# Recurrence level products as paired 64-column halves, both live units in one block ahead of the probability-value batch

## The chip, the cores and the metric

The kernel runs on one core of a Trainium2 chip. TensorE (PE in the profile, its weight loads PEld) multiplies matrices into PSUM; VectorE (DVE) and ScalarE (ACT) read PSUM and SBUF; GpSimd (POOL) works on SBUF; SyncE (SP) issues the DMAs here. Each engine runs its own queue in order and waits on semaphores for the others. The metric is the device time of one execution in microseconds.

## The reference, cut to what matters

One transformer layer over 2048 latent tokens with 256 context tokens in front: a modulated norm, one input projection, two groups of heads side by side, an output projection, then a feed-forward part. The change lies where the two groups of heads are computed together:

```python
# (A) softmax attention: 8 query heads, 2 key/value heads, 128-query blocks, 2304 keys
s = einsum('bqkgd,bnkd->bkgqn', q, keys) * scale;  p = softmax(s);  o = einsum('bkgqn,bnkd->bqkgd', p, vals)
# (B) gated linear recurrence: 4 heads of 128 x 128, forward and backward, chunks of 64
S_t = diag(f_t) S_{t-1} + k_t v_t^T ;  o_t = S_t^T q_t       # k = 1 - f, f the forget gate
o = rmsnorm(o_forward + o_backward) * silu(g)
```

Inside a chunk of the recurrence the score of a query and a key is multiplied by the product of the forget gates between them. The kernel builds those products by doubling: level `lv` treats blocks of `2**lv` tokens, and after seven levels a block is 128 tokens.

## The kernel before

The stage works through 64 items, each a pair of query heads in one block of 128 queries; a **round** is one pass of the loop over `work` (class `Pair`). A round makes six score tiles `s` (128 x 768, `L817`) for its own item and, between them, nine groups `pt` of four transposes (`L840`) for the item before. At its end it multiplies that item's transposed probabilities with the values in one batch `av` (`L853`). Per `s` tile DVE finds the row minimum `neg` (`L820`) and ACT takes the exponential `pr` (`L825`). Two PSUM buffers hold the `s` tiles (`N_S`), so a tile can be written once the exponential of the tile two before it is done. ACT and DVE copy the transposes out as `pf` (`L846`, `L844`). POOL rescales two thirds of each head's probabilities (`L832`).

The recurrence is cut into 20 **units**: for each of four heads a context unit of 256 tokens (unit 0) and four units of 512. A unit loads its gates `F`, makes `M` and `C` (products of gates, forward and backward) and a query copy `Q`, forms the product `pd` for the diagonal (`L629`, copied to `A` by ACT, `L630`), and goes through seven levels. A level of a 512-token unit multiplies four 128 x 128 blocks of `M` with columns of `Q` into `pa` (`L640`), lets DVE merge them into `A` under a mask (`L643`), and then updates `M`, `C` and `Q` (POOL `L652`, `L655`, `L664`, `L666`; ACT copies `L658`, `L659`) and the short gate products `T` (DVE `L671`). Then two transposes `pk` (`L680`), the forward product `psf` with a chain of four state updates `S` on DVE (`L694`), and the backward product `psb` (`L699`). When the five units of a head are done, `head_out` forms `po` four times (`L730` to `L732`) and normalizes it: ACT squares it, DVE sums, POOL takes a power, DVE multiplies and so reads `po` last (`L738`, `L740`, `L123`, `L742`, `L747`).

All of `pd`, `pa`, `pk`, `psf`, `psb` and `po` use one PSUM buffer (`ps_h`, `N_H` = 1): each waits for the last reader of the one before it. `recurrence()` keeps two units live and takes a step of each in turn; a round calls it in five places, so that 4.4 steps a round stand between the score tiles:

```python
                if j != 4:
                    other()
            if prev is not None:
                prev.products()
```

PE's order is the order of the program text; the orders of the other engines are made by a scheduler from the same program. POOL's, DVE's and ACT's queues thus hold attention and recurrence work mixed.

Of the kernel before, what the change touches and what calls it, by code (L numbers as in the profile page):

```python
# [30 lines left out]
ROT = 1000  # L31
# [16 lines left out]
SLOTS, STEPS = 5, 4.4  # L48
# [22 lines left out]
def block_kernel(ctx: ExitStack, tc: tile.TileContext, a: dict, out: bass.AP, dbg=None):  # L71
# [499 lines left out]
    with ExitStack() as st:  # L571
# [22 lines left out]
        nrot = [0]  # L594

        def rot():

            nrot[0] += 1
            return nc.vector if nrot[0] % ROT == 0 else nc.gpsimd

        def hg_unit(h, u, V, S, units):

            n = 256 if u == 0 else 512
            nch = n // P
            t0 = 0 if u == 0 else 256 + (u - 1) * 512
            F = up.tile([P, 512, 2], F32, tag="F", name=f"F{h}{u}", bufs=2)
            nc.sync.dma_start(F[:, :n, :].rearrange("p t d -> p (t d)"),
                              s_f[h][:, t0 * 2:(t0 + n) * 2])
            M = up.tile([P, 512], F32, tag="M", name=f"M{h}{u}_0", bufs=4)
            C = up.tile([P, 512], F32, tag="C", name=f"C{h}{u}_0", bufs=4)  # L610
            pair = "p (j s) -> p j s"
            nc.scalar.activation(M[:, :n].rearrange(pair, s=2), strided(F[:], 0, [[4, n // 2], [3, 2]]),
                                 AF.Identity, scale=-1.0, bias=1.0)
            nc.scalar.activation(C[:, :n].rearrange(pair, s=2), strided(F[:], 1, [[4, n // 2], [1, 2]]),
                                 AF.Identity, scale=-1.0, bias=1.0)
            A = Q = None
            if u:
                A = kp.tile([P, 512], F32, tag="A", name=f"A{h}{u}", bufs=5)
                Q = kp.tile([P, 2, 512], F32, tag="Q", name=f"Q{h}{u}", bufs=5)
                q = up.tile([P, 512], F32, tag="q", name=f"q{h}{u}", bufs=2)  # L620
                nc.sync.dma_start(q, s_hq[h][:, (u - 1) * 512:u * 512])
                kk = up.tile([P, 512], F32, tag="o", name=f"kk{h}{u}", bufs=2)
                nc.gpsimd.tensor_tensor(kk, M, C, op=ALU.add)
                for d in range(2):
                    getattr(nc, QI).tensor_tensor(Q[:, 1 - d, :], q, F[:, :, d], op=ALU.mult)
                pa = ps_h.tile([P, 512], F32, tag="h", name=f"pd{h}{u}")
                for c in range(nch):
                    cs = slice(c * P, (c + 1) * P)
                    nc.tensor.matmul(pa[:, cs], kk[:, cs], q[:, cs], start=True, stop=True)  # L629
                nc.scalar.activation(A, pa, AF.Copy)  # L630
            yield
            Tt = F
            for lv in range(7):
                hs = 1 << lv
                nb = n // hs
                if u:
                    pa = ps_h.tile([P, 512], F32, tag="h", name=f"pa{h}{u}{lv}")
                    for c in range(nch):
                        cs = slice(c * P, (c + 1) * P)
                        nc.tensor.matmul(pa[:, cs], M[:, cs],  # L640
                                         strided(Q[:], c * P, [[2 * hs, 64 // hs], [512 + hs, 2], [1, hs]]),
                                         start=True, stop=True)
                    nc.vector.copy_predicated(  # L643
                        A.rearrange("p (c t) -> p c t", t=P),
                        mask[:, lv, None, :].to_broadcast([P, 4, P]),
                        pa.rearrange("p (c t) -> p c t", t=P))
                M2 = up.tile([P, 512], F32, tag="M", name=f"M{h}{u}_{lv + 1}", bufs=4)
                C2 = up.tile([P, 512], F32, tag="C", name=f"C{h}{u}_{lv + 1}", bufs=4)
                if nb >= 4:
                    g4 = nb // 4  # L650
                    odim = [[4 * hs, g4], [3 * hs, 2], [1, hs]]
                    rot().tensor_tensor(strided(M2[:], 0, odim), strided(M[:], 0, odim),  # L652
                                        strided(Tt[:], 2, [[8, g4], [3, 2], [0, hs]]), op=ALU.mult)
                    idim = [[4 * hs, g4], [hs, 2], [1, hs]]
                    rot().tensor_tensor(strided(C2[:], hs, idim), strided(M[:], hs, idim),  # L655
                                        strided(Tt[:], 1, [[8, g4], [5, 2], [0, hs]]), op=ALU.mult)
                    cdim = [[4 * hs, g4], [1, 2 * hs]]
                    nc.scalar.activation(strided(M2[:], hs, cdim), strided(C[:], hs, cdim), AF.Copy)  # L658
                    nc.scalar.activation(strided(C2[:], 0, odim), strided(C[:], 0, odim), AF.Copy)  # L659
                if u:  # L660
                    Q4 = Q.rearrange("p d (j s h) -> p d j s h", s=2, h=hs)
                    T3 = Tt[:, :nb, :].rearrange("p (j s) d -> p j s d", s=2)
                    sh = [P, nb // 2, hs]
                    rot().tensor_tensor(Q4[:, 1, :, 1, :], Q4[:, 1, :, 1, :],  # L664
                                        T3[:, :, 0, 0][:, :, None].to_broadcast(sh), op=ALU.mult)
                    rot().tensor_tensor(Q4[:, 0, :, 0, :], Q4[:, 0, :, 0, :],  # L666
                                        T3[:, :, 1, 1][:, :, None].to_broadcast(sh), op=ALU.mult)
# [4 lines left out]
                M, C, Tt = M2, C2, T2  # L672
                yield

            KTs = []
            for d in range(2):
                pk = ps_h.tile([P, 512], F32, tag="h", name=f"pk{h}{u}{d}")
                for c in range(nch):
                    src = (M, C)[(c + d) % 2]
                    nc.tensor.transpose(pk[:, c * P:(c + 1) * P], src[:, c * P:(c + 1) * P], ident)  # L680
                kt = up.tile([P, 512], F32, tag="kt", name=f"kt{h}{u}{d}", bufs=4)
                nc.scalar.activation(kt[:, :n], pk[:, :n], AF.Copy)
                KTs.append(kt)
                yield
            ps = ps_h.tile([P, 512], F32, tag="h", name=f"psf{h}{u}")
            for c in range(nch):
                nc.tensor.matmul(ps[:, c * P:(c + 1) * P], KTs[0][:, c * P:(c + 1) * P],
                                 V[:, t0 // P + c, :], start=True, stop=True)
            for c in range(nch):
                g = t0 // P + c  # L690
                if g == 0:
                    nc.vector.tensor_copy(S[:, 1, :], ps[:, :P])
                else:
                    nc.vector.scalar_tensor_tensor(S[:, g + 1, :], S[:, g, :], Tt[:, c, 0:1],  # L694
                                                   ps[:, c * P:(c + 1) * P], op0=ALU.mult, op1=ALU.add)
            yield
            ps = ps_h.tile([P, 512], F32, tag="h", name=f"psb{h}{u}")
            for c in range(nch):
                nc.tensor.matmul(ps[:, c * P:(c + 1) * P], KTs[1][:, c * P:(c + 1) * P],  # L699
                                 V[:, t0 // P + c, :], start=True, stop=True)  # L700
            dSb = kp.tile([P, 4, P], F32, tag="dS", name=f"dS{h}{u}")
            nc.scalar.activation(dSb[:, :nch, :].rearrange("p c v -> p (c v)"), ps[:, :n], AF.Copy)
            units[u] = A, Q, Tt, dSb
            yield

        def head_out(h, V, S, units):
            _, _, Tt, dSb = units[0]
            coef, add = [Tt[:, 0, 1:2], dSb[:, 1, :]], dSb[:, 0, :]

            def chain(u):  # L710
# [3 lines left out]
                for c in range(3, -1, -1):  # L714
# [3 lines left out]
                    coef, add = [units[u][2][:, c, 1:2], Sb], units[u][3][:, c, :]  # L718
# [5 lines left out]
            for u in range(4, 0, -1):  # L724
                A, Q, Tt, dSb = units[u]
# [26 lines left out]
        def recurrence():  # L752

            def stream():
                for h in range(NH):
                    V = hp.tile([P, NTOK // P, P], F32, tag="V", name=f"V{h}", bufs=2)
                    nc.sync.dma_start(V, s_i[h // 2][:, (h % 2) * P:(h % 2 + 1) * P]
                                      .rearrange("(t p) v -> p t v", p=P))
                    S = hp.tile([P, NTOK // P + 1, P], F32, tag="S", name=f"S{h}")
                    units = {}  # L760
                    for u in range(5):
                        yield hg_unit(h, u, V, S, units), None
                    yield head_out(h, V, S, units), units
            pending = stream()
            live = []
            more = True
            while live or more:
                while more and len(live) < LIVE:
                    nxt = next(pending, None)
                    if nxt is None:  # L770
                        more = False
                        break
                    gen, units = nxt
                    if units is not None:
# [130 lines left out]
        for item in work + [None]:  # L905
# [64 lines left out]
            for j, n in enumerate((2, 1, 2, 2, 1, 1)):  # L970
# [6 lines left out]
                if j != 4:  # L977
                    other()
# [484 lines left out]
```

## Time and profile before

| | |
|---|---|
| three runs | 3467.97, 3469.89, 3483.88 us (median 3469.89) |
| profiled execution | 3474.03 us, its span 3472.3 us, mean granted clock 0.983 |
| the attention stage | 722.4 to 1912 us of the span, 64 rounds |
| PE busy over the whole span | 3283.9 us (95%) |

A row of groups reads: line, engine, operation, output<-inputs, shapes, count | busy us, mean ns of one | idle time before them, and what ended it. A row of a timeline reads: start us, length us, engine, line, operation, and in brackets the idle time before it and its releaser. A matmul in full fp32 (`pa`, `pd`, `psf`, `psb`, `po`, `av`) leaves two records; a transpose and an `s` product leave one. Records of PE overlap, so the step from one group's start to the next one's start is the time that it takes.

### The profile page before, as it was taken

The page shows a single profiled execution, that of the slowest core. Times are in us where ns is not written, and L with a number is a line of the kernel's source. Part 1 is how long each engine was busy: PE and PEld are TensorE (multiplying, and loading weights), DVE is VectorE, ACT ScalarE, POOL GpSimd, SP SyncE. Part 2 cuts the span into 40 slices and gives each one's busy share as a digit, 9 for nine tenths or more (in the row PEclk, how much of TensorE's full clock was granted, in tenths as well). Part 3 has the DMA queues.
Part 4 walks back from the last instruction along what each step waited for, and adds up shares of the span by engine and source line. Part 5 has one row for each costly group of instructions (what it writes and reads, how often), then busy time and mean ns, then how long its engine had stood idle before and what let it go on. Part 6 is the DMA issues. An engine that isn't in the chain of part 4 may idle for free. (4 is left out here: it accounts for less than half of the span.)

```text
span 3472.3 us, 53309 instructions
## 1 busy us (share of the span) xinstructions
PE 3283.9 (95%) x19324; PEld 2736.6 (79%) x19324; DVE 1938.0 (56%) x3302; ACT 1605.6 (46%) x3343; POOL 1785.8 (51%) x1616
## 2 busy tenths in 40 slices
PE   8999999979999899999998999999989989999998
PEld 5998987967777777777776887788867768888887
DVE  6444555146676776676666557444456663333566
ACT  4322222247767666776665214333334443333444
POOL 4322232047768767776775106866642257666322
PEclk9999999989999999999999999999989999999999
DMA  7344655431121103001003433544475543232664
GB/s 234 96 136 136 178 159 177 120 92 32 32 56 45 32 28 94 26 29 56 26 22 110 145 126 107 174 155 153 149 246 187 176 146 117 93 103 94 238 208 164
DMA packets 358616, 407.94 MB, mean 117 GB/s; under 512 B 31856, under 2 KB 249936, under 8 KB 358096
## 3 DMA queue, kind: packets, MB, share of 16 engines
q1 hardware_dynamic: 358352, 404.53, 36.7%
q8 instruction: 152, 2.49, 0.3%
q14 instruction: 112, 0.92, 0.1%
HBM read 274.92 MB, written 129.52 MB: 116 GB/s over the span
## 5 line engine op out<-in xcount | busy, mean ns | idle before, releaser
L832 POOL TENSOR_TENSOR pr<-pr,fac 128x768 f32<-128x768 f32 x256 | 374.4, 1484 | 215.2 <-DMA mf<-in_k_mask_dram 101.8
L820 DVE TENSOR_REDUCE neg<-s 128x1 f32<-128x768 f32 x384 | 365.2, 954 | 198.6 <-PE s L817 198.0
L817 PE MATMUL s<-K,qs 128*128 128x512 f32 (+1 forms) x1536 | 372.1, 365 | 34.5 <-ACT pr L825 30.9
L825 ACT ACTIVATE pr<-s,neg 128x768 f32<-128x768 f32 x384 | 348.2, 907 | 75.2 <-DVE neg L824 38.9
L817 PEld LDWEIGHTS s<-K,qs 128*128 128x128 f32 x1536 | 264.4, 192 | 105.5 <-ACT pr L825 43.7
L840 PE MATMUL pt<-identr,pr 128*128 128x128 f32 x2304 | 321.0, 275 | 12.3 <-ACT pf L846 7.4
L846 ACT ACTIVATE pf<-pt 128x512 f32<-128x512 f32 x448 | 256.7, 600 | 108.2 <-PE pt L840 106.3
L840 PEld LDWEIGHTS pt<-identr,pr 128*128 128x128 f32 x2304 | 261.8, 141 | 21.7 <-ACT pf L846 12.5
L853 PE MATMUL av<-pf,V 128*64 128x256 f32 x2304 | 266.1, 385 | 1.5 <-DVE pf L844 1.5
L853 PEld LDWEIGHTS av<-pf,V 128*64 128x64 f32 x2304 | 161.2, 138 | 87.0 <-issue 7.8
L1354 POOL TENSOR_TENSOR y<-y,yg 128x512 f32<-128x512 f32 x48 | 76.1, 1600 | 287.0 <-DVE yg L1353 283.2
L640 PE MATMUL pa<-Q,M 128*128 128x128 f32 x896 | 131.3, 291 | 30.8 <-POOL Q L666 17.1
L1323 DVE TENSOR_TENSOR x<-lr,x 128x512 fp32r<-128x512 f32 x154 | 119.8, 813 | 67.5 <-ACT x L1322 64.6
L1323 DVE TENSOR_TENSOR dl<-lr,dh 128x512 fp32r<-128x512 f32 x154 | 118.6, 808 | 68.2 <-ACT dh L1322 68.2
L640 PEld LDWEIGHTS pa<-Q,M 128*128 128x128 f32 x896 | 116.3, 195 | 38.8 <-POOL Q L666 20.7
L1322 ACT ACTIVATE dh<-lr 128x512 fp32r<-128x512 f32 x154 | 89.5, 623 | 113.0 <-PE pd1A L1377 55.0
L1322 ACT ACTIVATE x<-lr 128x512 fp32r<-128x512 f32 x154 | 90.7, 626 | 93.7 <-PE pd0A L1377 38.5
L345 PE MATMUL f<-hTh,wh 128*128 128x512 f32 (+1 forms) x320 | 121.1, 379 | 4.9 <-ACT ft L374 4.9
L1184 PE MATMUL pA<-x,A11h 128*128 128x512 f32 x352 | 113.3, 402 | 9.3 <-ACT A11h L1157 7.8
L1377 PE MATMUL pd0A<-x,x 128*128 128x512 f32 x528 | 120.7, 389 | 0.0
L345 PE MATMUL f<-hTh,wl 128*128 128x512 f32 (+1 forms) x320 | 119.3, 373 | 0.0
L345 PE MATMUL f<-hTl,wh 128*128 128x512 f32 (+1 forms) x320 | 118.8, 371 | 0.0
(331 smaller groups left out, 9188.7 us busy)
## 6 DMA issues: line engine op xcount, KB each, us to landing
w<-in_w_gu_dram SPq DMA_DIRECT2D x88, 512.0 KB
wm<-in_w_mod_dram SPq DMA_DIRECT2D x24, 1024.0 KB
lr<-s_wT SPq DMA_DIRECT2D x88, 256.0 KB
lr<-in_w_down_dram SPq DMA_DIRECT2D x66, 256.0 KB
s_q<-sq SPq DMA_DIRECT2D x128, 128.0 KB
qs<-s_q SPq DMA_DIRECT2D x32, 512.0 KB
wq<-in_w_down_dram SPq DMA_DIRECT2D x44, 256.0 KB
s_wT<-wq SPq DMA_DIRECT2D x44, 256.0 KB
```

Of the source, the lines that this page charges most:

```text
L345: nc.tensor.matmul(pm[:, :n], w[wi][:, k, c0:c0 + P], hT[b][hi][:, k, :], start=(k == 0 and i == 0), stop=(k == KT - 1 and i == 2))
L640: nc.tensor.matmul(pa[:, cs], M[:, cs], strided(Q[:], c * P, [[2 * hs, 64 // hs], [512 + hs, 2], [1, hs]]), start=True, stop=True)
L817: nc.tensor.matmul(s[:, o:o + w], self.qs[:, hh, self.item[2], half, :], self.kv[0][:, k0 + o:k0 + o + w], start=(half == 0), stop=(half = ...
L820: nc.vector.tensor_reduce(neg[:, i:i + 1], s[:, :n], axis=AX.X, op=ALU.min)
L825: nc.scalar.activation(pr[:, k0:k0 + n], s[:, :n], AF.Exp, bias=neg[:, m:m + 1], scale=-1.0, accum_out=self.ls[:, hh, i:i + 1])
L832: nc.gpsimd.tensor_tensor(pj, pj, self.fac[:, hh, j:j + 1].to_broadcast([P, SW]), op=ALU.mult)
L840: nc.tensor.transpose(pt[:, (2 * i + hh) * P:(2 * i + hh + 1) * P], self.prs[hh][:, (2 * k2 + i) * P:(2 * k2 + i + 1) * P], ident)
L846: nc.scalar.activation(pf, pt, AF.Copy)
L853: nc.tensor.matmul(self.av[i * 64:(i + 1) * 64], self.kv[1][:, 2 * k2 + i, :], self.pf[k2][:, i * 256:(i + 1) * 256], start=(n == 0), stop ...
L1322: nc.scalar.activation(hi, src, AF.Copy)
L1323: nc.vector.tensor_tensor(lo, src, f32v(hi), op=ALU.subtract)
L1377: nc.tensor.matmul(cur[t], l[:, t * P:(t + 1) * P], r, start=(start and j == 0 and f == 0), stop=(stop and j == NHF - 1 and f == 2), skip_ ...
```

## The change

A level's product is cut by columns. Instead of four matmuls of 128 output partitions by 128 columns, a unit issues eight of 64 output partitions by 64 columns, the two halves of a block to partitions 0 to 63 and 64 to 127 of the same PSUM columns. Two units then fill one PSUM tile. The levels leave the five places between the score tiles: once a round, after the last transposes, the level products of both live units stand together in front of the `av` batch, and the rest of the level (merge, updates) is issued behind that batch. Units start at fixed rounds (1, 4, 8, 11, 15, ...), a unit's `pd` takes the place of the step at `j == 5` of its first round, and the context units run beside the others without PE work. What is left for the places between the score tiles are the closing steps (`pk`, `psf`, `psb`, `po`), which are now taken one unit after another. The gate tile `F` and `q` have one buffer instead of two.

```diff
-                    for c in range(nch):
-                        cs = slice(c * P, (c + 1) * P)
-                        nc.tensor.matmul(pa[:, cs], M[:, cs],
-                                         strided(Q[:], c * P, [[2 * hs, 64 // hs], [512 + hs, 2], [1, hs]]),
-                                         start=True, stop=True)
+                for c in range(self.nch):
+                    for i in range(2):
+                        if hs < 64:
+                            q = strided(self.Q[:], c * P + i * 64, [[2 * hs, 32 // hs], [512 + hs, 2], [1, hs]])
+                        else:
+                            q = self.Q[:, 1 - i, c * P + (1 - i) * 64:c * P + (2 - i) * 64]
+                        nc.tensor.matmul(pa[i * 64:(i + 1) * 64, c * 64:(c + 1) * 64],
+                                         self.M[:, c * P + i * 64:c * P + (i + 1) * 64], q,
+                                         start=True, stop=True)
...
+                self.starts = {1 + 7 * (n // 2) + 3 * (n % 2): n for n in range(4 * NH)}
...
+            def round(self):
+                live = [(i, self.lanes[i]) for i in sorted(self.lanes)]
+                if not live:
+                    return
+                pa = ps_h.tile([P, 512], F32, tag="h", name=f"pa{live[0][1].h}{live[0][1].u}{live[0][1].lv}")
+                for i, u in live:
+                    u.scores(pa[:, i * 256:(i + 1) * 256])
+                yield
+                for i, u in live:
+                    u.level(pa[:, i * 256:(i + 1) * 256])
+                    if u.lv == 7:
+                        del self.lanes[i]
+                yield
...
-                if j != 4:
-                    other()
+                if j == 1:
+                    rec.prepare(r)
+                if j != 4 and not (j == 5 and rec.diagonal(r)):
+                    rec.step()
+                if j != 5:
+                    next(rec.beside, 0)
+            made = rec.round()
+            next(made, 0)
             if prev is not None:
                 prev.products()
+            next(made, 0)
```

What that does to PE's order is seen at the last level of a unit. Before, it stands between two score tiles (`pa036` is head 0, unit 3, level 6; `s1_4_0_1_0` is a score tile):

```order
L840 MATMUL pt4_0_0_7_9623<-identr_107,pr4_0_0_0_9392 128x128
L840 MATMUL pt4_0_0_7_9623<-identr_107,pr4_0_0_1_9497 128x128
L640 MATMUL pa036_9630<-Q03_8906,M03_6_9526 128x128 x4
L817 MATMUL s1_4_0_1_0_9646<-K0_7843,qs4_0_9388 128x512 x2
L817 MATMUL s1_4_0_1_0_9646<-K0_7843,qs4_0_9388 128x256 x2
```

Now units 3 and 4 share one tile, between a round's last transposes and the batch `av`:

```order
L934 MATMUL pt6_0_1_5_10673<-identr_107,pr6_0_1_0_10356 128x128
L934 MATMUL pt6_0_1_5_10673<-identr_107,pr6_0_1_1_10429 128x128
L648 MATMUL pa036_10680<-Q03_9360,M03_6_10523 64x64 x8
L648 MATMUL pa036_10680<-Q04_9988,M04_3_10534 64x64 x8
L947 MATMUL av6_0_1_10697<-pf6_0_1_6_10566,V0_7848 64x256 x2
L947 MATMUL av6_0_1_10697<-pf6_0_1_7_10573,V0_7848 64x256 x2
```

The second place is the first `po` of a head on PE. Before, score tiles and transposes follow it:

```order
L730 MATMUL po04_10640<-V0_7867,A04_10016 128x128
L731 MATMUL po04_10640<-S0_7869,Q04_10017 128x128
L732 MATMUL po04_10640<-Sb0_12_10587,Q04_10017 128x128
L817 MATMUL s1_7_0_0_0_10672<-K0_7843,qs7_0_10610 128x512 x2
L817 MATMUL s1_7_0_0_0_10672<-K0_7843,qs7_0_10610 128x256 x2
```

Now it is the last step of round 19, and the next user of `ps_h`, with `av` behind it, follows directly:

```order
L748 MATMUL po04_11817<-V0_7909,A04_9987 128x128
L749 MATMUL po04_11817<-S0_9397,Q04_9988 128x128
L750 MATMUL po04_11817<-Sb0_12_11783,Q04_9988 128x128
L648 MATMUL pa114_11849<-Q11_10804,M11_4_11643 64x64 x8
L648 MATMUL pa114_11849<-Q12_11490,M12_1_11654 64x64 x8
L947 MATMUL av9_0_0_11866<-pf9_0_0_6_11680,V0_7848 64x256 x2
```

The third place is DVE's queue where the context unit of head 1 begins (`T10_0` to `T10_6` are its gate products, `neg` the row minima). Before, they stand apart, one between two minima:

```order
L820 TENSOR_REDUCE neg3_0_1_0_9160<-s0_3_0_1_0_9161 128x1
L671 TENSOR_TENSOR T10_0_10760<-F10_10697 128x256
L643 COPY_PREDICATED A02_8853<-mask_7819,pa022_9182 128x512
L820 TENSOR_REDUCE neg3_0_1_0_9160<-s1_3_0_1_0_9198 128x1
L875 TENSOR_TENSOR oo2_0_1_9219<-pof2_0_1_9212,li2_0_1_9216 128x256
```

Now eight `T` operations stand in a row in front of the first minimum of round 16:

```order
L658 COPY_PREDICATED A04_9987<-mask_7819,pa110_10918 128x512
L967 RECIPROCAL li7_0_1_11263<-li7_0_1_11263 128x2
L686 TENSOR_TENSOR T10_0_11042<-F10_11005 128x256
L686 TENSOR_TENSOR T10_1_11075<-T10_0_11042 128x128
L686 TENSOR_TENSOR T11_1_11195<-T11_0_10965 128x256
L686 TENSOR_TENSOR T10_2_11106<-T10_1_11075 128x64
L686 TENSOR_TENSOR T11_2_11413<-T11_1_11195 128x128
L686 TENSOR_TENSOR T10_3_11128<-T10_2_11106 128x32
L686 TENSOR_TENSOR T10_4_11243<-T10_3_11128 128x16
L686 TENSOR_TENSOR T10_5_11276<-T10_4_11243 128x8
L914 TENSOR_REDUCE neg8_0_0_0_10983<-s0_8_0_0_0_10984 128x1
```

The load of `F10` itself now waits until unit 1's level 0 has read the single `F` buffer.

More of the change, by code (lines that the diff above doesn't have):

```diff
@@ L689, in hg_unit @@
[L689 to L704, printed above, removed]
+                nc.scalar.activation(kt[:, :self.n], pk[:, :self.n], AF.Copy)
+                self.kt[d] = kt
+            def forward(self, V, S):
+                ps = ps_h.tile([P, 512], F32, tag="h", name=f"psf{self.h}{self.u}")
+                for c in range(self.nch):
+                    nc.tensor.matmul(ps[:, c * P:(c + 1) * P], self.kt[0][:, c * P:(c + 1) * P],
+                                     V[:, self.t0 // P + c, :], start=True, stop=True)
+                for c in range(self.nch):
+                    g = self.t0 // P + c
+                    if g == 0:
+                        nc.vector.tensor_copy(S[:, 1, :], ps[:, :P])
+                    else:
+                        nc.vector.scalar_tensor_tensor(S[:, g + 1, :], S[:, g, :], self.T[:, c, 0:1],
+                                                       ps[:, c * P:(c + 1) * P], op0=ALU.mult, op1=ALU.add)
@@ new lines, in backward @@
+            def backward(self, V):
+                ps = ps_h.tile([P, 512], F32, tag="h", name=f"psb{self.h}{self.u}")
+                for c in range(self.nch):
+                    nc.tensor.matmul(ps[:, c * P:(c + 1) * P], self.kt[1][:, c * P:(c + 1) * P],
+                                     V[:, self.t0 // P + c, :], start=True, stop=True)
+                self.dS = kp.tile([P, 4, P], F32, tag="dS", name=f"dS{self.h}{self.u}")
+                nc.scalar.activation(self.dS[:, :self.nch, :].rearrange("p c v -> p (c v)"), ps[:, :self.n], AF.Copy)
@@ L750, in head_out @@
                 yield
[L752 to L774, printed above, removed]
-                        while len(units) < 5:
-                            for g in list(live):
-                                if next(g, 0) == 0:
-                                    live.remove(g)
-                                else:
-                                    yield
-                    live.append(gen)
-                for g in list(live):
-                    if next(g, 0) == 0:
-                        live.remove(g)
-                    else:
-                        yield
@@ L888, in block_kernel @@
         work = [(qt, g, hp2) for g in range(2) for qt in range(NCH) for hp2 in range(2)]
[L889 to L899 removed]
+        rec = Recurrence()
         prev = done = None
@@ L904, in block_kernel @@
         border.enter_context(tc.manual_schedule(engines={mybir.EngineType.PE}))
-        for item in work + [None]:
+        for r, item in enumerate(work + [None]):
+            rec.begin(r)
             if item is None:
-                while rec is not None:
-                    other()
+                assert not rec.lanes
+                while rec.steps:
+                    rec.step()
                 order_T = iter(T_ORDER)
```

223 lines of the change are left out of this document (145 added, 78 removed).

## The prediction

> **What bounds the kernel now.** I read the busy shares by stretch first, then the groups and the waits inside the attention stage, then the timelines of single rounds. The stretch from 722.4 to 1912 us is the stage that changes; outside it nothing does.
>
> ```profile
> 722.40:1912.00 1189.60, 1076.27 (x8112) 896.10 (x8111) 803.12 (x1359) 805.32 (x1830) 852.87 (x907) 0.98 0.17 49
> L817 PE MATMUL s<-K,qs x1536: 274/387/794, 724.7 to 1898.0; 128*128 128x512 f32 x192
> L817 PE MATMUL s<-K,qs 128*128 128x512 f32 (+1 forms) x1536 | 372.1, 365 | 34.5 <-ACT pr L825 30.9 <-DMA qs<-s_q 2.4
> L640 PE MATMUL pa<-Q,M 128*128 128x128 f32 x896 | 131.3, 291 | 30.8 <-POOL Q L666 17.1 <-DVE S L694 8.6 <-ACT kt L682 3.1
> L820 DVE TENSOR_REDUCE neg<-s 128x1 f32<-128x768 f32 x384 | 365.2, 954 | 198.6 <-PE s L817 198.0
> L643 DVE COPY_PREDICATED A<-mask,pa 128x512 f32<-128x512 int32 x112 | 83.3, 744 | 52.7 <-PE pa L640 52.5
> L694 DVE SCALAR_TENSOR_TENSOR S<-S,T,psf 128x128 f32<-128x128 f32 x68 | 23.4, 344 | 9.9 <-PE psf L687 8.8
> PE psb L699 <- DVE S L694: 6.0, 5, 1.3
> PE po L730 <- DVE o L747: 4.8, 3, 2.3
> L630 ACT ACTIVATE A<-pd x15: 597/607/677, 830.3 to 1753.4; 128x512 f32<-128x512 f32 x15
> ```
>
> PE (first pair of figures) is busy 1076 of 1190 us; the next engine, POOL (the last pair), 853. So PE is the bound, and it idles only 113 us. A round takes 18.4 us in the mean (the second row: 1898.0 less 724.7, over almost 64 rounds). The groups and waits say where PE idles: 30.8 us ahead of `pa`, of which 17.1 for POOL's update of `Q` and 8.6 for the state chain, 34.5 ahead of score tiles. The change can win only in those 113 us and in what `pa` itself costs.
>
> A round without a level shows the floor:
>
> ```profile
> 1035.92 0.97 PE L817 MATMUL s<-K,qs 128*128 128x512 f32 x4
> 1036.73 1.03 PE L840 MATMUL pt<-identr,pr 128*128 128x128 f32 x8
> 1037.52 0.95 PE L817 MATMUL s<-K,qs 128*128 128x512 f32 x4
> 1038.31 0.60 PE L840 MATMUL pt<-identr,pr 128*128 128x128 f32 x4
> ...
> 1039.44 0.97 PE L817 MATMUL s<-K,qs 128*128 128x512 f32 x4 [0.31 <-ACT pr L825]
> ...
> 1046.08 4.11 PE L853 MATMUL av<-pf,V 128*64 128x256 f32 x36
> 1050.11 0.97 PE L817 MATMUL s<-K,qs 128*128 128x512 f32 x4
> ```
>
> From `s` at 1035.92 to `s` at 1050.11 are 14.19 us, with four stray transposes of `pk` in it (0.4 us at the pace of `pt`). So a bare round takes 13.8 us, and already there a score tile waits 0.31 us for the exponential two tiles back: with little between them, score tiles run at the pace of DVE and ACT.
>
> **The change, term by term.** Each term is a change of the stage against the profiled execution (3474.03 us; the median of the runs is 4.1 us lower).
>
> *1. The level products themselves: -21 us (-51 to +99).*
>
> ```profile
> 1225.29 1.06 PE L640 MATMUL pa<-Q,M 128*128 128x128 f32 x8
> 1226.10 0.94 PE L817 MATMUL s<-K,qs 128*128 128x512 f32 x4
> ```
>
> Eight records of 128 columns take 0.81 us to the next start, 0.9 with the tail that `s` then waits out; 112 levels make 101 us. Afterwards there are 1792 records of 64 columns. The nearest row is `av`, which also writes two halves of 64 partitions: 36 records of 256 columns in 4.03 us, 224 ns a pair. If a pair scales with its columns it takes 56 ns, 50 us in all: -51. If a record costs what one of 128 columns costs now (0.9/8 = 112 ns), it is 200 us: +99. I take 45 ns a record, 80 us: `av` shows that halves overlap, but four times as many instructions per column have to be fed. The Trainium skill ("TensorE: Matmul & The Clock Gate", Back-to-back issue gap) speaks against the cut: it gives about 81 ns for each pair of weight load and matmul in a stream at 128 columns. By that figure an estimate of the products would be 145 us, +44 here; no row here has pairs that short, so the trace neither confirms nor excludes it.
>
> *2. Waits of the old levels: -31 us.* The 30.8 us ahead of `L640` go, since `M` and `Q` now have a whole round to get ready. What is late next at that place are terms 5 and 7. The merges (0.744 us each on DVE) and updates move under `av`, 4.03 us, which hides them; and `F` and `q` of the 512-token units are loaded a round ahead, so their single buffer costs nothing.
>
> *3. The start: -17 us.*
>
> ```profile
> 730.49 1.65 PE L817 MATMUL s<-K,qs 128*128 128x512 f32 x4 [4.16 <-ACT pr L825]
> 745.05 2.08 PE L629 MATMUL pd<-q,kk 128*128 128x128 f32 x8 [12.92 <-DVE T L671]
> ```
>
> The first `pd` stands at the end of round 1 now, not in round 0: the 12.9 us and most of the 4.2 go.
>
> *4. Score tiles in rounds that have no steps: +10 us (0 to +30).* By the order, 30 rounds have nothing left but `s`, `pt`, `pa` and `av`. At 0.6 us a round (the 0.31 twice) they wait 18 us, up to 40 if minima or exponentials queue. Of today's 30.9 us some 10 are such waits, the rest a few long ones (4.16 above, 7.90 below).
>
> *5. `pd` directly ahead of `pa`: +11 us (+11 to +30).* In the first round of each of 16 units ACT must empty the single `ps_h` between the two, with `av` queued behind. The copy takes 0.607 us, with a semaphore 0.7; 16 of them are 11 us, and up to 30 if an exponential goes first.
>
> *6. Closing steps one after another: +15 us (+5 to +25).* After `psf` DVE does four `S` of 0.344 us with a minimum of 0.954 among them, while `psb` is now the very next step, one score tile and eight transposes or 1.6 us later (1035.92 to 1037.52). Where the two met like that today the wait was up to 1.3 us; 16 x 1.3 = 21, less the 6.0 paid now.
>
> *7. `po` directly ahead of `pa` or `po`: +42 us (+20 to +55).*
>
> ```profile
> 1271.85 0.39 PE L732 MATMUL po<-Sb,Q 128*128 128x128 f32 x2
> 1272.27 0.60 ACT L738 ACTIVATE o<-po 128x512 f32<-128x512 f32 x1 [1.19 <-PE po L732]
> 1277.18 0.68 DVE L740 TENSOR_REDUCE sso<-o 128x4 f32<-128x512 f32 x1
> 1279.74 1.05 POOL L123 TENSOR_TENSOR rs_o<-ms_o,mhalf 128x4 f32<-128x4 f32 x1 [4.39 <-DVE ms_o L121]
> 1281.02 0.69 DVE L747 TENSOR_TENSOR o<-po,rs_o 128x512 f32<-128x512 f32 x1
> 998.29 0.39 PE L732 MATMUL po<-Sb,Q 128*128 128x128 f32 x2
> 1002.84 0.69 DVE L747 TENSOR_TENSOR o<-po,rs_o 128x512 f32<-128x512 f32 x1
> 1845.99 0.49 PE L730 MATMUL po<-V,A 128*128 128x128 f32 x2 [2.30 <-DVE o L747]
> 1208.22 2.89 POOL L832 TENSOR_TENSOR pr<-pr,fac 128x768 f32<-128x768 f32 x2
> ```
>
> From the end of `po` at 1272.24 to its last read at 1281.71 are 9.5 us through four engines; the other instance here, from 998.68, takes 4.9. The chain's own work is 3.0 us and two short instructions; the rest is queueing behind minima, exponentials and POOL's pairs of 2.89 us. Today other work covers it but for 4.8 us. In three heads `pa`, with `av` behind it, now stands right behind the first `po`, and POOL's queue there holds such a pair and two `Q` products first: 8.5 us of the chain are exposed. The second `po` meets the third after two score tiles and sixteen transposes, 3.2 us: the 2.3 us seen at 1845.99, where two of them meet in the same way. The third meets `pa` after two tiles and eight transposes, 2.5 us: about 3.2. So 14 x 3 = 42; with every chain at 4.9 it is 3 x (4.9 + 1.7 + 2.4) = 27 or, where one is covered by chance, 20. The last head's four `po` stand as before.
>
> *8. Gate products of a context unit ahead of a minimum: +30 us (0 to +50).*
>
> ```profile
> 1203.40 9.45 DVE L671 TENSOR_TENSOR T<-F 128x512 f32<-128x512 f32 x1 [0.54 <-POOL Q L666]
> 1199.21 2.56 POOL L625 TENSOR_TENSOR Q<-q,F 128x512 f32<-128x512 f32 x2
> ...
> 1211.66 0.64 POOL L655 TENSOR_TENSOR C<-M,T 128x256 f32<-128x256 f32 x1
> 1214.36 0.90 ACT L825 ACTIVATE pr<-s,neg 128x768 f32<-128x768 f32 x1 [7.56 <-DVE neg L820]
> 1215.40 1.65 PE L817 MATMUL s<-K,qs 128*128 128x512 f32 x4 [7.90 <-ACT pr L825]
> 738.34 4.93 DVE L671 TENSOR_TENSOR T<-T 128x128 f32<-128x128 f32 x5
> 731.51 0.42 SPq L607 DMA_DIRECT2D F<-s_f  x1
> 736.66 0.66 ACT L612 ACTIVATE M<-F 128x512 f32<-128x512 f32 x1 [0.94 <-DMA F<-s_f]
> ```
>
> In the first row DVE's product ends only when POOL's run of fourteen instructions (first and last row shown) has ended at 1212.3. Minimum, exponential and PE came late in turn, 7.90 us. Five smaller products with POOL busy took 4.93 us. The Trainium skill ("SBUF — State Buffer", where it describes the shared port pair) says that a VectorE instruction with two SBUF inputs and a GpSimd instruction exclude each other for a whole instruction; the 9.45 us agree. Now eight such products stand in a row ahead of the first minimum of rounds 16, 30 and 44, and others around round 2. The first needs a load that starts only when unit 1's level 0 has released `F`, and in SP's queue behind that of `q`; a load took 5.1 us from issue to use (731.51 to 736.66), so it lands after `av`, when POOL is full of `Q`, `M` and `C`; eight products at about 1 us follow. 7 to 9 us in each of four places are 30; if POOL happens to be idle, nothing.
>
> *9. The rest: -3 us.* The old 7.90 us goes with its cause. Long waits also lower the clock for a few us (behind the 7.90 four `s` take 1.65 us where 0.94 is usual): six new ones at 2 us, +12, less 7 at the start.
>
> Sum: -21 - 31 - 17 + 10 + 11 + 15 + 42 + 30 - 3 = +36. Waits of one round shadow each other (terms 4 to 6 together are 36); I take 6 off. **+30 us**: the profiled execution at 3504, the median at 3500 us.
>
> **The rivals.** *A, the gains stay and the clumps are covered.* Halves overlap fully (-51), waits and start go (-48), the old 7.90 goes (-8), the `po` chains cost their least (+20), the load lands early (0), 4 to 6 cost 22. That is -65; with a third of it missed -45, so 3425 us. For it speaks that other engines catch up while PE waits, and that 30 rounds would take 15.2 us (13.8 and 1.4 of products) against 18.4 in the mean. Against it, 16 closing rounds of 21 us (15.2, 3.6 of steps, 2 of waits) and six of 26 to 29 around `po` give that back. *B, feeding binds.* At 78 ns a record, half way between my value and today's 112, the products take 140 us and the time is 3560. From 56 ns on, term 1 is a loss. The `av` rows speak against it, the doubled count of instructions for it. The rule of the skill in term 1 would be a case of this rival. *C, nothing measurable.* Terms 7 and 8 at about half, the rest as summed: 3470 us.
>
> **How the numbers follow.** Forecast 0.43, A 0.27, C 0.18, B 0.12. About 0.5%, 17 us, is what a measurement of this kernel can tell from no change. So faster 0.27, same 0.18, slower 0.55. The forecast's own range is 3487 to 3535. The whole range reaches down to A's 3425, which leaves out half of A, and up to 3565, past B's 3560 and past the forecast with terms 7 and 8 at their upper ends (3533) and no gain in term 1 (3554).
>
> **What would show it.** Right: PE waits 5 to 10 us for `o` ahead of the level product of rounds 19, 33 and 47; the first exponential of rounds 16, 30 and 44 is late behind `T`; rounds without steps take about 15.3 us; the level products take 60 to 110 us. Wrong: 32 records in under 1.1 us together with `po` waits under 4 us (A), or over 2.2 us (B); or a wait I have not priced, above all transposes waiting for POOL's rescaling, which by the order now stands behind the round's `Q` updates.

## The result, and the profile after

The changed kernel takes 3507.14 us (median of 6 runs, 3494.28 to 3509.73), the kernel before 3474.48 us (6 runs): a ratio of 1.0087, 95% interval 1.0065 to 1.0109. It is slower by 33 us; the forecast was 3500, and +30 for the stage.

The profiled execution took 3509.73 us. The two rows below are the stage itself in both kernels, from the first score tile's start to the last one's end (columns: stretch, length, busy us and instructions of PE, weight loads, DVE, ACT and POOL, granted clock, DMA share, GB/s). First before, then after:

```profile
724.70:1898.40 1173.70, 1060.37 (x7999) 883.24 (x7998) 794.70 (x1348) 797.95 (x1815) 845.81 (x903) 0.98 0.16 48
```

```profile
732.70:1934.30 1201.60, 1045.11 (x8896) 856.78 (x8895) 768.20 (x1348) 798.49 (x1817) 845.13 (x903) 0.96 0.16 46
```

The stage is 27.9 us longer. PE is busy 15.3 us less in it and idles 156.5 us instead of 113.3. Another 8.0 us lie ahead of the stage, where the program is the same: its first score tile starts at 732.7 instead of 724.7 us. In the waits of PE ahead of the stage this is mostly one line, the input projection waiting for a copy (before, then after):

```profile
PE f L345 <- ACT ft L374: 4.9, 4, 1.7
```

```profile
PE f L343 <- ACT ft L372: 10.6, 5, 3.3
```

In the profiles of the kernels below that start lies between 718.4 and 728.4 us, whatever their order, so those 8 us are put down to the execution and not to the change. Kernels are compared below by the length of the stage in their profiles, beside the medians of their runs. Each kernel has one profile, and its stage can differ from the median run's: for the sixth kernel below by about 20 us.

What PE waits for in the stage after the change (total us, times, longest):

```profile
PE s L911 <- ACT pr L919: 50.3, 61, 4.5
PE pa L648 <- DVE o L765: 33.6, 9, 7.6
PE psb L719 <- DVE S L712: 15.5, 12, 1.3
PE po L748 <- DVE o L765: 14.9, 5, 3.5
PE pa L648 <- ACT A L636: 13.3, 16, 1.3
```

The old waits of the level product, 17.1 us for `Q` and 8.6 for `S`, are gone. The two for `o`, 48.5 us together, are new but for the 4.8 that `po` paid before. A round without steps shows the new level block between the last transposes and `av` (timeline of PE):

```profile
843.87 0.60 PE L934 MATMUL pt<-identr,pr 128*128 128x128 f32 x4
844.39 1.15 PE L648 MATMUL pa<-Q,M 128*64 128x64 f32 x32
845.38 4.06 PE L947 MATMUL av<-pf,V 128*64 128x256 f32 x36
```

32 records take 0.99 us to the next start, 31 ns each: two levels for little more than one cost before (0.81 to 0.9). Over the stage, counting each record up to the next one's start, the level products fell from 107.6 to 60.7 us. The first `po` of a head, and the level block right behind it:

```profile
1076.81 0.39 PE L750 MATMUL po<-Sb,Q 128*128 128x128 f32 x2
1083.76 1.98 PE L648 MATMUL pa<-Q,M 128*64 128x64 f32 x32 [6.57 <-DVE o L765]
1085.50 5.67 PE L947 MATMUL av<-pf,V 128*64 128x256 f32 x36
...
1076.03 3.01 POOL L926 TENSOR_TENSOR pr<-pr,fac 128x768 f32<-128x768 f32 x2 [2.98 <-ACT fac L922]
1079.00 2.56 POOL L629 TENSOR_TENSOR Q<-q,F 128x512 f32<-128x512 f32 x2
1081.67 1.01 POOL L121 TENSOR_TENSOR rs_o<-ms_o,mhalf 128x4 f32<-128x4 f32 x1
...
1082.92 0.69 DVE L765 TENSOR_TENSOR o<-po,rs_o 128x512 f32<-128x512 f32 x1
```

The four-element power `rs_o` on POOL stands behind 5.6 us of other work, and all of PE behind it. Then PE also runs slow: the block takes 1.74 us to the next start, `av` 5.6 instead of 4.0.

### The profile page after: what moved, and what is told of

Its sections match the earlier page's. It is cut to its first block, busy times and chain, and to the rows that moved or that the text cites. A ratio compares the mean times of both kernels' runs of the same rounds, so it can differ in the third digit from the quotient of the medians.

```text
span 3507.9 us, 54970 instructions
## 1 busy us (share of the span) xinstructions
PE 3272.7 (93%) x20220; PEld 2714.0 (77%) x20220; DVE 1906.7 (54%) x3302; ACT 1605.0 (46%) x3343; POOL 1784.7 (51%) x1616
## 5 line engine op out<-in xcount | busy, mean ns | idle before, releaser
L911 PE MATMUL s<-K,qs 128*128 128x512 f32 (+1 forms) x1536 | 380.4, 371 | 54.5 <-ACT pr L919 50.3
L934 PE MATMUL pt<-identr,pr 128*128 128x128 f32 x2304 | 328.2, 280 | 13.7 <-DVE oo L969 6.5
L934 PEld LDWEIGHTS pt<-identr,pr 128*128 128x128 f32 x2304 | 269.4, 144 | 21.6 <-ACT pf L940 7.8
L947 PEld LDWEIGHTS av<-pf,V 128*64 128x64 f32 x2304 | 170.8, 142 | 74.9 <-issue 4.6
L121 POOL TENSOR_TENSOR rs_qq<-ms_qq,mhalf 128x4 f32<-128x4 f32 x32 | 35.2, 1102 | 160.3 <-DVE ms_qq L119 155.7
L1469 PEld LDWEIGHTS pd0A<-x,x 128*128 128x128 f32 x528 | 99.1, 188 | 20.6
```

The costliest lines, as they stand in the source:

```text
L911: nc.tensor.matmul(s[:, o:o + w], self.qs[:, hh, self.item[2], half, :], self.kv[0][:, k0 + o:k0 + o + w], start=(half == 0), stop=(half = ...
L934: nc.tensor.transpose(pt[:, (2 * i + hh) * P:(2 * i + hh + 1) * P], self.prs[hh][:, (2 * k2 + i) * P:(2 * k2 + i + 1) * P], ident)
L947: nc.tensor.matmul(self.av[i * 64:(i + 1) * 64], self.kv[1][:, 2 * k2 + i, :], self.pf[k2][:, i * 256:(i + 1) * 256], start=(n == 0), stop ...
L1469: nc.tensor.matmul(cur[t], l[:, t * P:(t + 1) * P], r, start=(start and j == 0 and f == 0), stop=(stop and j == NHF - 1 and f == 2), skip_ ...
```

## Experiments: the two parts apart

The first kernel is the one before, with the halves and nothing else:

```diff
-                    for c in range(nch):
-                        cs = slice(c * P, (c + 1) * P)
-                        nc.tensor.matmul(pa[:, cs], M[:, cs], strided(Q[:], c * P, ...), start=True, stop=True)
+                    for c in range(nch):
+                        for i in range(2):
...
+                            nc.tensor.matmul(pa[i * 64:(i + 1) * 64, c * 64:(c + 1) * 64],
+                                             M[:, c * P + i * 64:c * P + (i + 1) * 64], qh,
+                                             start=True, stop=True)
```

> The kernel before, with its level products cut into 64-column halves and nothing else: same places, one unit at a time, PSUM buffer and step order as before. Theory: the halves are a plain gain. In the changed kernel 1792 records of 64 columns took 60.7 us where 896 of 128 took 107.6, so PE should need 47 us less here too, and the waits ahead of the level product (30.8 us, 17.1 of them for the update of Q) stay: about 3430 us, level products near 60 us. Rival: the recurrence's chain through POOL and DVE sets the pace of a level, so that a shorter product only makes PE wait longer for Q; half of the gain is lost, the waits ahead of the level product grow to 50 us or more, 3450 to 3460 us. Second rival: the gain needs the 32 records in one block; in blocks of 16 the fill and drain eat it, 3465 us or more.

3463.82 us against 3475.74, ratio 0.9966 (0.9951 to 0.9980); the stage is 1158.2 us, 15.5 less than before. By the medians the gain is 12 us, and the profiled execution was the fastest of nine. That is a quarter to a third of the 47 that the theory wanted. Waits of its PE, and two of its level products on PE's timeline:

```profile
PE s L821 <- ACT pr L829: 28.9, 38, 7.3
PE pa L644 <- POOL Q L670: 19.8, 12, 3.6
...
1085.75 1.04 PE L844 MATMUL pt<-identr,pr 128*128 128x128 f32 x8
1086.71 0.70 PE L644 MATMUL pa<-Q,M 128*64 128x64 f32 x16
1087.35 0.97 PE L821 MATMUL s<-K,qs 128*128 128x512 f32 x4
...
1089.30 0.60 PE L844 MATMUL pt<-identr,pr 128*128 128x128 f32 x4
1089.83 0.69 PE L644 MATMUL pa<-Q,M 128*64 128x64 f32 x16
1090.34 4.06 PE L857 MATMUL av<-pf,V 128*64 128x256 f32 x36
```

The level products fell by 34.8 us by their own records, but the rest of PE's work grew by 14.0 and its idle time by 5.3. The first rival has a part in that: the waits ahead of the level product are 40.8 us instead of 30.8, 2.7 of it for `Q` and most of the rest one wait of 6.8 for `A`. The second rival is right in its mechanism and too pessimistic in size: a block of 16 pays to get in and out. From the last transpose's start to the block's first record pass 0.20 us (0.53 less three steps of 0.109 between transposes), where a block of full width needs one step of 0.11. From its first record, 0.64 us pass until a score tile starts and 0.51 until `av`, which works in halves too. In the median of the blocks without a wait a level costs 0.203 + 0.615 = 0.82 us, where it cost 0.109 + 0.873 = 0.98 before: 0.16 x 112 = 18 us. In the changed kernel two levels share one entry and go straight into `av`: 0.203 + 0.983 = 1.19 us for two, 0.59 for one. So the pairing, and the place ahead of `av`, bring more of the matmul gain than the halves by themselves.

The second kernel is the changed one with its old width:

```diff
-                    for i in range(2):
...
-                        nc.tensor.matmul(pa[i * 64:(i + 1) * 64, c * 64:(c + 1) * 64],
-                                         self.M[:, c * P + i * 64:c * P + (i + 1) * 64], q, ...)
+                    nc.tensor.matmul(pa[:, cs], self.M[:, cs], strided(self.Q[:], c * P, ...),
+                                     start=True, stop=True)
...
-                    u.scores(pa[:, i * 256:(i + 1) * 256])
+                    u.scores(pa)
```

> The changed kernel with its level products at the old width: each unit's four matmuls of 128 by 128, both units into the same PSUM columns one after the other (the second overwrites the first, so the scores it merges are not the reference's). Order, steps and waits are those of the changed kernel. Theory: the block costs 16 records at 112 ns, 1.8 us, where it costs 1.0 now; 112 levels make 101 us against 61, so 40 us more than the changed kernel, about 3547 us, step-free rounds 15.6 us instead of 14.8. Rival: a record's cost hangs on its weight load and issue, not on its columns; 16 records then cost less than 32 and the time falls below 3507 us.

3535.92 us against 3475.74, ratio 1.0173 (1.0153 to 1.0193); 29 us above the changed kernel's median, the stage 1234.4 us, 32.8 above. Its step-free rounds take 15.6 us, as expected:

```profile
855.32 0.60 PE L930 MATMUL pt<-identr,pr 128*128 128x128 f32 x4
855.76 1.95 PE L644 MATMUL pa<-Q,M 128*128 128x128 f32 x16
857.64 4.11 PE L943 MATMUL av<-pf,V 128*64 128x256 f32 x36
```

16 records take 1.88 us where 32 halves take 0.99. Columns decide, not records: both blocks push 2048 columns, and the halves, which go to different output partitions, pass two at a time (the two of a pair start 7 ns apart, the next pair 58 ns after). Over the stage the theory's 40 us for the level products were too few: by their own records they take 124.2 us, 63.5 more than in the changed kernel, because a block behind a wait costs 2.4 to 3.7 us. What remains is 32.8 because the rest of PE's work fell by 15 us and its idle time by as much (141.1 us against 156.5).

The two kernels make a table of four (stage, us): before 1173.7; halves alone 1158.2; the new order alone 1234.4; both 1201.6. The order by itself costs 61 us and the halves give 33 of them back. What remained was to find what in the order costs so much.

## Experiments: what the order costs

The third kernel frees the single PSUM buffer early:

```diff
-                nc.scalar.activation(o, po, AF.Square)
+                oc = up.tile([P, 512], F32, tag="kt", name=f"oc{h}{u}", bufs=4)
+                nc.scalar.activation(oc, po, AF.Copy)
+                nc.scalar.activation(o, oc, AF.Square)
...
-                nc.vector.tensor_tensor(o3, p3, rs[:, :, None].to_broadcast([P, 4, P]), op=ALU.mult)
+                nc.vector.tensor_tensor(o3, oc.rearrange("p (c v) -> p c v", v=P),
+                                        rs[:, :, None].to_broadcast([P, 4, P]), op=ALU.mult)
```

> The changed kernel, with po copied out of PSUM by ACT (one more ACTIVATE of 128x512 for each of 16 po) and the square and the last product reading the copy, so that the PSUM buffer is free after the copy. Theory: the waits for o ahead of the level product and of the next po (33.6 and 14.9 us) shrink to a copy of 0.6 us and what stands ahead of it on ACT, 14 times about 1 us: 34 us less; the clock in the six slow rounds comes back to 1.0, another 10 to 15: about 3460 us, rounds 19 and 20 at 21 to 24 us instead of 31. Rival: the waits were short-lived cover for another late thing (score tiles waiting for exponentials queued behind po's chain on DVE and ACT), which now shows; 15 us less, 3492 us.

3447.71 us against 3475.74, ratio 0.9924 (0.9907 to 0.9942): 59 us below the changed kernel, where the theory wanted 47, and 28 below the kernel before. The stage is 1145.2 us, 56.4 below. Of the 48.5 us of waits for `o` only a wait for the copy is left; rounds 19 and 20 follow (the changed kernel's, then this one's):

```profile
PE pa L648 <- ACT oc L756: 2.1, 3, 0.7
```

```profile
1059.60:1091.10 31.50, 22.07 (x164) 18.29 (x163) 17.11 (x28) 13.91 (x33) 23.39 (x26) 0.84 0.19 53
1091.10:1121.90 30.80, 23.56 (x181) 20.89 (x179) 16.78 (x30) 13.10 (x28) 13.98 (x15) 0.83 0.13 37
```

```profile
1047.50:1068.40 20.90, 18.18 (x164) 15.04 (x162) 13.67 (x25) 14.04 (x33) 16.43 (x17) 1.00 0.17 55
1068.40:1087.90 19.50, 19.36 (x180) 16.67 (x178) 16.99 (x26) 12.97 (x28) 15.10 (x19) 1.00 0.17 46
```

The same 164 PE instructions are busy 18.2 us at a granted clock of 1.00 and 22.1 us at 0.84. Over the stage, idle time fell by 41.8 us and busy time by 14.6: a long wait is paid twice. The rival's late score tiles do show, in rounds 21, 35 and 49, which wait 2.0 us for an exponential and grow from 17.7 us to between 21.2 and 21.7. But all score waits together are where they were (50.2 us), because rounds 37 and 51 lost theirs of 4.5.

The fourth kernel tests the context unit's gate products:

```diff
+                        self.ctx[n // 4] = Unit(n // 4, 0)
+                        self.ctx[n // 4].load()
...
-                self.F = up.tile([P, 512, 2], F32, tag="F", name=f"F{h}{u}", bufs=1)
+                self.F = up.tile([P, n, 2], F32, tag="F" if u else "gt", name=f"F{h}{u}", bufs=1)
```

> The changed kernel, with the context unit's gate tile in a buffer of its own (that of gt) and its load issued a round earlier; the scheduler then puts its gate products T ahead of round 15 instead of ahead of the first minimum of round 16 (the same in the other heads). Theory: the 2.9 us waits for an exponential in rounds 16, 30 and 44 and the clock of 0.91 behind them go: these rounds fall from 19.7 to about 15.6 us, 12 us in all, and rounds 1 to 3 gain a little: about 3494 us. Rival: the T products take the same DVE and POOL time wherever they stand, and delay minima in the round before by as much: no change, 3507 us.

3504.96 us, ratio 1.0090 (1.0070 to 1.0110): no gain, as the rival said. By its profile the stage is even longer, 1213.0 us against 1201.6. In the changed kernel round 16 took 19.7 us (first row, clock 0.91). With the early load it takes 16.2, but round 13, to which the scheduler moved the products (not to round 15), takes 18.9 instead of 14.8:

```profile
1002.60:1022.30 19.70, 15.96 (x132) 12.90 (x130) 16.57 (x30) 14.16 (x38) 17.24 (x23) 0.91 0.12 32
```

```profile
940.40:959.30 18.90, 15.92 (x132) 12.85 (x130) 14.06 (x22) 11.87 (x26) 12.16 (x15) 0.91 0.11 33
994.40:1010.60 16.20, 14.70 (x132) 11.43 (x130) 11.96 (x20) 12.71 (x33) 16.04 (x22) 1.00 0.11 34
```

The three that follow build on the third kernel. The fifth moves the products to POOL:

```diff
-                nc.vector.tensor_tensor(T2, T3[:, :, 0, :], T3[:, :, 1, :], op=ALU.mult)
+                (nc.vector if u else nc.gpsimd).tensor_tensor(T2, T3[:, :, 0, :], T3[:, :, 1, :], op=ALU.mult)
```

> The kernel of the third experiment (po copied out), with the gate products T of the four context units on POOL instead of DVE; all else, their place in the program too, as there. Theory: the first minimum of rounds 16, 30 and 44 no longer stands behind T on DVE; those rounds fall from 19.8 to about 16.5 us, with a little in rounds 1 to 3: 10 us less than the third experiment, about 3438 us. Rival: it isn't the T products on DVE but POOL's whole run of context work that holds DVE and ACT (its M, C and Q products), so the score waits stay: 3448 us.

3444.63 us, 3 below the third kernel, within the spread of both (3437.17 to 3446.84 and 3443.22 to 3453.68). Rounds 16, 30 and 44 do fall, from 19.8 to 17.0 us in the mean, so the products on DVE were what the first minimum waited for. But rounds 18, 32 and 46 grow from 20.3 to 20.7 us to 21.5, and PE's score waits are 51.9 us where the third kernel had 50.2. A queue shortened at one place is long at the next.

The sixth gives two of the closing steps other buffers:

```diff
-                pa = ps_h.tile([P, 512], F32, tag="h", name=f"pd{self.h}{self.u}")
+                pa = ps_t2.tile([P, 512], F32, tag="t", name=f"pd{self.h}{self.u}")
...
-                ps = ps_h.tile([P, 512], F32, tag="h", name=f"psb{self.h}{self.u}")
+                ps = ps_t2.tile([P, 512], F32, tag="t", name=f"psb{self.h}{self.u}")
```

> The kernel of the third experiment, with pd and psb written into the two rotating PSUM buffers of the transposes instead of the single buffer; the order of the steps is the same. Theory: the 13.3 us that the level product waits for the copy of pd and the 15.5 us that psb waits for the state chain are due to the single buffer alone and go; the transposes two groups later wait a little for the copies of pd and psb, some 6 us: 22 us less than the third experiment, about 3426 us. Rival: the wait only changes its name, each of the 36 pd and psb now holds a transpose for a copy of 0.6 us: 8 us less, 3440 us.

3427.64 us, 20 below the third kernel and near the theory's 3426. Its profile does not show this gain: the profiled execution took 3447.78 us where its other five took 3418.99 to 3429.24, and its stage is 1145.1 us, as long as the third kernel's. One wait stands out in it, twice as long as in the next kernel:

```profile
PE pt L936 <- DVE oo L971: 25.0, 10, 4.4
```

So the waits are read from the seventh kernel, which has both edits:

> Both of the edits above on the kernel of the third experiment. Theory: the gains add, 32 us less than the third experiment, about 3416 us. Rival: the score tiles at DVE's and ACT's pace take back what the single buffer cost: 3435 us.

3427.36 us, ratio 0.9870 (0.9853 to 0.9888): the sixth kernel's gain alone. The fifth's adds nothing that the runs can tell, so neither the theory's 3416 nor the rival's 3435 came. The stage is 1123.4 us, and its waits are:

```profile
PE s L913 <- ACT pr L921: 35.3, 53, 4.2
PE pt L936 <- DVE oo L971: 12.3, 8, 2.1
PE psb L719 <- ACT pf L942: 11.3, 20, 0.7
PE pt L936 <- ACT pf L942: 10.0, 13, 1.4
PE pk L696 <- ACT kt L698: 9.0, 20, 1.5
PE pof L965 <- ACT dS L722: 8.1, 4, 2.0
```

The size of the two new buffers' gain came out as expected, the way did not. The 13.3 us for `A` and the waits for `S` (15.5 ahead of `psb`, 3.5 ahead of `pd`) are gone, and 19.4 us for `pf` and `dS` have taken their place; the transposes wait 25.4 us where the fifth kernel has 18.6. That is some 6 us net, about the 8 that the sixth kernel's rival said. The rest lies in the score waits, 35.3 us where the fifth kernel has 51.9. Why they fell was not tested. These two kernels are the fastest of the study, 1.3% below the kernel before.

## Why the prediction was right

The sign, the size and the largest cause were right. The terms that are waits add up to +46 us, and PE idles 43.2 longer; those that are PE's own work add up to -16, and it is 15.3 shorter. The first sum is a forecast that held, with a miss in it. The second is luck: terms 1 and 9 were mis-sized by about 26 us each, in opposite directions.

- **Term 1, level products (-21 us):** mis-sized. They measured -47 by their own records, of which 5.5 go back at the entry to 59 blocks (0.09 us each). I took 45 ns a record and got 31 to 34. `av` had been the right row, and its pace scaled by columns (my bound of -51) the one that came true; the allowance for instructions that must be fed was not needed. By the Trainium skill ("TensorE: Matmul & The Clock Gate", Back-to-back issue gap), whose 81 ns a pair are for 128 columns, the estimate was 145 us; the trace has 61.
- **Term 2, old waits (-31):** right. No level product waits for `Q`, `S` or `kt` any more. But its last clause, that the single buffer of `F` costs nothing, failed. In rounds 9, 23, 37 and 51 DVE idles 1.0, 1.0, 5.2 and 5.2 us for the `F` of a 512-token unit, the gate products of that unit stand ahead of minima in its queue, and PE waits 2.5 and 2.5 us at transposes, 4.5 and 4.5 at score tiles. The last two are the longest score waits of the stage, and I priced none of the four. In round 37:

```profile
1435.21 0.75 DVE L686 TENSOR_TENSOR T<-F 128x512 f32<-128x512 f32 x1 [5.22 <-DMA F<-s_f]
1436.00 3.00 DVE L686 TENSOR_TENSOR T<-T 128x256 f32<-128x256 f32 x3
1438.92 1.82 DVE L914 TENSOR_REDUCE neg<-s 128x1 f32<-128x768 f32 x2
1440.95 1.65 PE L911 MATMUL s<-K,qs 128*128 128x512 f32 x4 [4.53 <-ACT pr L919]
```

  SP issues that load at 1431.58 us, just when POOL's read of the `F` before it ends. No run gave `F` its second buffer back, so what this costs in all stays open.
- **Term 3, the start (-17):** the wait of 12.9 us went, that of 4.2 did not (4.09 us now). Round 0 fell from 30.5 to 14.9 us also because its `pd` and its level stand in round 1 now; the three rounds behind it gave 4.6 us back.
- **Terms 4 and 8, score tiles (+10 and +30):** the mechanism was right, term 8 was too large, and its longest waits came in rounds 37 and 51 (term 2). Of 25 rounds without steps and with two units, 15 wait 0.43 us, not 0.6; the other ten wait 1.2 to 3.7. All score waits went from 30.9 to 50.3 us; with the old 7.9 us gone, that is some 27 new against 40 forecast. The profile shows term 8 as told, on DVE in round 16:

```profile
1003.17 0.43 DVE L686 TENSOR_TENSOR T<-F 128x256 f32<-128x256 f32 x1 [2.24 <-DMA F<-s_f]
1003.64 3.66 DVE L686 TENSOR_TENSOR T<-T 128x128 f32<-128x128 f32 x7
1007.21 0.95 DVE L914 TENSOR_REDUCE neg<-s 128x1 f32<-128x768 f32 x1
...
1009.24 0.96 PE L911 MATMUL s<-K,qs 128*128 128x512 f32 x4 [2.86 <-ACT pr L919]
```

  The load is late and the products stand ahead of the minimum, but one takes 0.5 us, not 1, and the score tile waits 2.9 us, not 7 to 9. The Trainium skill's exclusion of the two engines ("SBUF — State Buffer", the shared port pair) shows little in these: seven products take 3.66 us, 0.52 each, with POOL busy beside them for most of it, where one product of before took 9.45.
- **Term 5 (+11):** right, 13.3 us in 16 waits.
- **Term 6 (+15):** 9.5 us; 12 of the 16 units paid their 1.29 us, 15.5 in all, against 6.0 before.
- **Term 7, `po` (+42):** right, 48.5 less 4.8 is 43.7. The waits of rounds 19, 33 and 47 were 6.57, 7.62 and 7.34 us (8.5 forecast), in rounds 20, 34 and 48 about 3.5 and 3.7 (3.2 each). The third experiment shows the cause.
- **Term 9, the clock (-3):** the step that failed. I set 12 us for slow matmuls behind long waits, less 7 for those that go at the start. But all of PE's work apart from the level products is 31.6 us longer (984.0 against 952.4 of steps), of which the block entries are 5.5. The clock covers nearly all of the rest. In the clock record of these traces the granted clock in the stage is 1.0 or 0.5, never between; a round's 0.91 is the mean of a short stretch of 0.5 and a long one of 1.0, as in round 16:

```profile
1002.60:1010.20 7.60, 4.46 (x30) 3.67 (x29) 6.36 (x14) 4.55 (x13) 5.14 (x9) 1.00 0.26 73
1010.20:1013.60 3.40, 3.40 (x16) 3.21 (x15) 3.33 (x4) 3.40 (x10) 3.40 (x4) 0.51 0.07 19
```

  PE is busy for 81.2 us of the stage at 0.5, where it was 32.2 before. Four records of `s` take 1.43 us at 0.5 and 0.80 at 1.0, so up to half of that time is lost: the difference costs up to 24.5 us by this estimate, close to the 26 to be explained. For the third kernel, which is busy for 49.2 us at 0.5, the same estimate gives up to 16.0 us less than for the changed one, and 14.6 were measured.

Rival A was right on the halves and wrong on the cover: 0.99 us for 32 records, but `po` waits of 7 us. Rival B is out, and so is C: the interval of the ratio leaves out 1. Forecast rounds of 15.3 without steps, 21 with closing steps and 26 to 29 with `po` came as 14.8 (most of them), 20.0 to 20.7 and 28.5 to 31.5. One of my signs of being wrong did come, a wait that I had not priced: the one for `F` under term 2. The transposes that I feared would wait for POOL's rescaling did not.

## What to carry to other kernels

A better matmul shape is worth what the order around it lets through: here the halves gave 12 to 15 us at the old place and the new order took 61. Most of that came back (56 us of the stage) with one copy: a tile that is read again at the end of a chain through four engines had held the only buffer that PE needed next. Ask of every PSUM tile who reads it last, and copy it out when that reader stands far down another engine's queue; sixteen copies of 0.6 us saved 59. Price a long wait of PE with the slow matmuls behind it too, a third more here (14.6 us beside 41.8).

## What the runs showed of the hardware

Matmuls of 64 output partitions passed two at a time even at 64 columns: 32 in 0.99 us, against 16 of 128 partitions and 128 columns in 1.88. Going from transposes of 128 partitions to such halves cost 0.20 us where going to a block of full width cost 0.11. From the first record of a block of 16 halves 0.64 us passed until a full-width tile started, and 0.51 until `av`, halves too; blocks of halves are worth joining.

In the attention stage the granted clock fell to 0.5 for 3.4 us or a whole multiple of it, and was 1.0 otherwise. A round with one wait of 2.9 us shows 0.91 in the mean, those with one of 4.5 us 0.85, and those with one of 6.6 to 7.6 us 0.84 to 0.88; the 1.29 us waits of the closing rounds left them at 1.00. But the length of a single wait does not settle it. A wait of 2.49 us left round 9 at 1.00 where one of 2.54 goes with 0.91 in round 23, one of 3.1 us left round 24 of the kernel before at 1.00, and rounds 2 and 3, with no wait above 1.23 us, show 0.90.
